# One-core two-block network in fp32 halves: two stage ends rebuilt and 1/sqrt by a polynomial

## The chip, the cores and the metric

One core of a Trainium2 chip runs the whole network, one launch per execution. The metric is the device time of one execution in microseconds (us). Engines are named as in the profile: PE is the matrix engine and PEld its weight loads, DVE the vector engine, ACT the scalar engine, POOL the general one; SP only issues transfers.

## The reference, cut to what matters

The input is x of 512 positions by 1024 channels. First block, two layers of: RMS norm, one projection, three mixers (axial attention, pooling, window attention), gates, an output projection; then RMS norm, up projection, 3-tap convolution, gated product, down projection. Second block: a conformer convolution module with its feed-forward, then keys and values for a dilated attention, that attention and its feed-forward. What the change touches is the norms and the ends of two stages:

```python
def rms_norm(x, g):
    y = x * lax.rsqrt(jnp.mean(x * x, axis=-1, keepdims=True) + EPS)
    return y * g

def conformer_conv_module(h, w_in, b_in, dw, dw_b, ln_g, ln_b, w_out, b_out):
    u = h @ w_in + b_in
    u = u[..., :D_MODEL] * jax.nn.sigmoid(u[..., D_MODEL:])
    u = causal_dwconv(u, dw, dw_b)          # 31 taps, one filter per channel
    u = jax.nn.silu(layer_norm(u, ln_g, ln_b))
    return u @ w_out + b_out
...
# every stage: x = x + rms_norm(y, post_gain); h = rms_norm(x, pre_gain)
```

## The kernel before, in words

Every matrix product is made of three PE passes: both operands are split into a high half (an ACT copy, line 301 for weights) and a remainder (a DVE subtraction, line 302), and the passes are high by high, high by remainder, remainder by high (`mm3`, lines 345 to 347, weights standing; `mm3_rows`, lines 555 to 557, activations standing). A pass over 512 columns follows the one before it after about 0.23 us. Weights come in units of eight 128 by 128 tiles in the order of a list (`PLAN`): SP loads a unit into one of three `raw` buffers (line 269), `split_to` splits it two units ahead of its use into one of four `w` buffers, or, for the units that a closing uses twice, into a `keep` buffer that a stage lends (`keeper`). `queue_behind` puts the splits of kept units behind an instruction that a stage has named for that engine in `self.behind`; `self.hold` is the first kept unit that may not be split yet.

The instructions are emitted by a planner: `mm3` and its like advance a clock by their planned time (`spend`), and generators (`spawn`, `tick`) put their work in when the clock has passed what they yielded (`CONV_TAP`, `NORM_SUM`, `NORM_NEXT` and so on). The framework then orders each engine's list once more before the program is built, by what it holds to be ready, with emission as the priority; at run time each engine works down its list in order and waits where an operand is missing.

`closing` ends a stage in two halves of 256 rows. After the products of half 0 the generator `norms` runs the post norm (squares on ACT, line 403; `rms`, lines 396 and 397; `inv_sqrt`, lines 367 to 373; the residual, line 432) and `pre_norm` the next norm (four squares, `rms`, `xn` on ACT and DVE, lines 473 and 477, then the transposes `htp`, line 488, and the split into `hh` and `hl`), while PE has half 1 to do; then `head` multiplies half 0 of the next stage while half 1 is normed. `inv_sqrt` is one guess from the bits of the value and three Newton steps, ten DVE instructions in a chain; `rms` puts two before them. `rope` uses `inv_sqrt` too. The last closing has `last_norm` for each of its last two row tiles: add (line 449), square (403), gain over 1024 columns in place (451), `rms`, result (454) and the transfer out. At the start there is no matrix product before the first `pre_norm`: two squares per row tile, `rms`, `xn`, `htp`.

The conformer's first part (`conv_inputs`): 16 projections give eight tiles of channels. Tiles 0 to 2 are convolved on DVE by 30 multiply-adds each (`tap_sums`, line 1325; the last one writes `vc`), emitted `CONV_TAP` apart. Tiles 3 to 7 go to PE (`conv`): the gated product `cu` (line 1293) is spread by 16 small transfers (line 1301) into `cup`, 72 matmuls (line 1349) run in four quarters `i`, DVE adds the bias into `vc` (line 1359), and after a yield of 1.5 four transposes (line 1366) turn it; an ACT copy (1369) and four `bn_stats` (1373) follow. When all eight tiles have their statistics: `bn_aggr` (1378), variance plus epsilon (1382), `inv_sqrt`, the shift (1384), the normalization of four row tiles of 1024 columns, two on ACT (1389) and two on DVE (1393). `silu_tiles` then transposes each tile of channels back (`ltp`, line 1236), applies Silu on ACT (`ct`, line 1241) and splits it into `ch` and `cl` for the closing `cm_w_out`.

The dilated attention (`dilated`, `dilated_heads`): eight heads; the first four units of the closing `w_o` are multiplied by `close_begin` while the last head is still worked on; the four kept units get their buffers from a pool that is opened after the heads' own pool is closed.

Of the kernel before, what the change touches and what calls it, by code (L numbers as in the profile page):

```python
# [35 lines left out]
DIN = 5888  # L36
EPS = 1e-6
NEG = -1e30
UNIT = 8
# [5 lines left out]

CONV_DVE, CONV_TAP = 3, 1.0
AX_LANES, AX_SOFTMAX, AX_NEXT, AX_PROB = 2, 5.5, 2.0, 1.7
# [177 lines left out]
class Kernel:  # L225
# [136 lines left out]
    def inv_sqrt(self, y, v):  # L362

        nc = self.nc
        shape = list(v.shape)
        a = self.sm.tile(shape, F32, tag="nwa", name="nwa", bufs=4)
        nc.vector.tensor_scalar(
            y.bitcast(I32), v.bitcast(I32), -0.5, 1597463007.0, op0=OP.mult, op1=OP.add
        )
        for _ in range(3):  # L370
            nc.vector.tensor_tensor(a, y, y, op=OP.mult)
            nc.vector.scalar_tensor_tensor(a, a, -0.5, v, op0=OP.mult, op1=OP.mult)
            nc.vector.scalar_tensor_tensor(y, a, 1.5, y, op0=OP.add, op1=OP.mult)

# [15 lines left out]
    def rms(self, sums):  # L390

        nc = self.nc
        n = sums.shape[1]
        v = self.sm.tile([P, 2], F32, tag="var", name="var", bufs=2)[:, :n]
        y = self.sm.tile([P, 2], F32, tag="rst", name="rst", bufs=4)[:, :n]
        nc.vector.tensor_tensor(v, sums[:, :, 0], sums[:, :, 1], op=OP.add)
        nc.vector.tensor_scalar(v, v, 1.0 / D, EPS, op0=OP.mult, op1=OP.add)
        self.inv_sqrt(y, v)
        return y

    def square(self, x, total):
        junk = self.sp.tile([P, S], F32, tag="junk", name="junk")
        self.nc.scalar.activation(junk, x, AF.Square, accum_out=total)  # L403

# [38 lines left out]
    def last_norm(self, t, banks, y, gain):  # L443

        nc = self.nc
        sums = self.sm.tile([P, 2, 2], F32, tag="sums", name="sums", bufs=4)[:, :1]
        halves = [(y[:, t, n * S : (n + 1) * S], slice(n * S, (n + 1) * S)) for n in range(2)]
        for n, (to, _) in enumerate(halves):
            nc.vector.tensor_tensor(to, to, banks[n], op=OP.add)
            self.square(to, sums[:, 0, n : n + 1])  # L450
        nc.vector.tensor_tensor(y[:, t], y[:, t], gain, op=OP.mult)
        rs = self.rms(sums)
        for n, (to, cols) in enumerate(halves):
            nc.vector.scalar_tensor_tensor(
                self.x[:, t, cols], to, rs[:, 0:1], self.x[:, t, cols], op0=OP.mult, op1=OP.add
            )
            queue = nc.scalar if n else nc.sync
            queue.dma_start(self.out[t * P : (t + 1) * P, cols], self.x[:, t, cols])

    def pre_norm(self, h, gain, wait=(0.0, 0.0)):  # L460
# [9 lines left out]
        for i in range(2):  # L470
# [5 lines left out]
            else:  # L476
                last = nc.scalar.activation(
                    xn[i], self.x[:, 2 * h + i], AF.Copy, scale=rs[:, i : i + 1]
                )
            if h == 0 and self.n_unit:  # L480
                self.behind[last.ins.engine] = last.ins
# [771 lines left out]
    def conv_inputs(self):  # L1253
# [54 lines left out]
        def tap_sums():  # L1308
            for j in range(CONV_DVE):
# [27 lines left out]
                summed.append(j)  # L1337

        def conv():
            for j in range(CONV_DVE, KD):  # L1340
# [5 lines left out]
                for i in range(4):  # L1346
                    w = mats[j][:, i]
                    for m in range(CONV_M):
# [4 lines left out]
                        )  # L1353
                    self.spend(CONV_M * 0.218)
                    yield 0.0
                if j + 2 < KD:
# [5 lines left out]
                )  # L1362
                yield 1.5
                pt = self.psum("a", "ctp")
                for i in range(4):
                    nc.tensor.transpose(pt[:, i * P : (i + 1) * P], vc[:, i], self.ident)
                self.spend(0.45)
                by = pt.rearrange("s (i q c) -> s q i c", i=4, q=4)
                nc.scalar.activation(
                    vt[:, :, j * P : (j + 1) * P].rearrange("s q (i c) -> s q i c", i=4), by, AF.Copy  # L1370
                )
                for q in range(4):
                    nc.vector.bn_stats(stats[:, q, j], by[:, q])
            while len(summed) < CONV_DVE:
                yield 0.3
            mv = self.sm.tile([P, 4, 2], F32, tag="lmv", name="lmv")
            for q in range(4):
# [8 lines left out]
            )  # L1386
            for q in range(4):
                if q % 2:
                    nc.scalar.activation(
                        vt[:, q], vt[:, q], AF.Identity, scale=rs[:, q : q + 1], bias=sh[:, q : q + 1]  # L1390
                    )
                else:
                    nc.vector.tensor_scalar(
                        vt[:, q], vt[:, q], mv[:, q, 0:1], rs[:, q : q + 1],
                        op0=OP.subtract, op1=OP.mult,
                    )

# [151 lines left out]
    def dilated(self):  # L1549
        with self.tc.tile_pool(name="dily", bufs=1, reuse_waits="tile") as yp:  # L1550
# [3 lines left out]
            gain = self.row(yp, "mix_post_g1")  # L1554
            begun = self.dilated_heads(xs)
            with self.tc.tile_pool(name="kept", bufs=1, side="right", reuse_waits="tile") as tp:
                self.keeper(tp, "wt", 4)
                y = tp.tile([P, 4, D], F32, tag="y", name="y")
                self.closing("w_o", 0, xs, y, gain, "ffn_pre_g1", begun=begun)

# [224 lines left out]
```

## Time and profile before

| what | us |
|---|---|
| median of 3 runs (lowest, highest) | 3178.2 (3178.11, 3181.9) |
| profiled execution, its time | 3177.36 |
| its span, first to last instruction | 3175.6 |
| granted clock of PE, mean over the span | 0.997 |

The profile lists for each engine what it did, and for each idle stretch of an engine what ended it. In a row of the timeline the columns are start, duration, engine, line, operation, output<-inputs, shapes, count, and in square brackets the idle time of the engine ahead of it and who ended that. Rows of one kind that follow each other are merged.

### The profile page before, as it was taken

What the parts mean: (1) busy time and instruction counts of PE and PEld (TensorE: products, weight loads), DVE (VectorE), ACT (ScalarE), POOL (GpSimd) and SP (SyncE); (2) the same over time, 40 slices, a digit from 0 to 9 for tenths busy, and PEclk for the clock granted to TensorE, in tenths of its full rate; (3) what the DMA queues carried; (4) which work ended last, traced back from release to release, by engine and by line L of the source; (5) the groups of instructions that cost most, each with busy time, mean ns of one, the idle gap of its engine ahead of it and who ended that gap; (6) DMA issues with size and microseconds to landing.
All of it is one profiled execution on the core that took longest, in us unless ns stands there. A gap on an engine that the chain in (4) does not pass through costs nothing. (4 is left out here: it accounts for less than half of the span.)

```text
span 3175.6 us, 40474 instructions
## 1 busy us (share of the span) xinstructions
PE 3103.4 (98%) x15764; PEld 2609.7 (82%) x15764; DVE 1828.9 (58%) x3337; ACT 1360.2 (43%) x2231; POOL 337.1 (11%) x350
## 2 busy tenths in 40 slices
PE   8999999999999999999999989999999999999998
PEld 7788888888878888888888878888888888888887
DVE  6778346455676754555556865456545545464555
ACT  5566244334456643444334244334533333353332
POOL 0211100000011111000000000000143333100000
PEclk9999999999999999999999999999999999999999
DMA  4222232333311223233324422333222222223332
GB/s 139 67 77 84 94 106 85 95 100 94 99 64 60 90 90 107 79 100 98 95 93 161 152 87 73 97 95 120 74 87 73 75 86 80 74 87 99 95 99 73
DMA packets 86543, 293.84 MB, mean 93 GB/s; under 512 B 11088, under 2 KB 13904, under 8 KB 86352
## 3 DMA queue, kind: packets, MB, share of 16 engines
q1 hardware_dynamic: 82896, 278.41, 27.4%
q10 hardware_dynamic: 3456, 12.85, 1.1%
q8 instruction: 124, 2.03, 0.3%
q14 instruction: 67, 0.55, 0.0%
HBM read 287.81 MB, written 2.10 MB: 91 GB/s over the span
## 5 line engine op out<-in xcount | busy, mean ns | idle before, releaser
L345 PE MATMUL mm<-hh,w 128*128 128x512 f32 (+1 forms) x2720 | 1051.3, 386 | 0.0
L347 PE MATMUL mm<-hh,w 128*128 128x512 f32 (+1 forms) x2720 | 1035.7, 381 | 0.0
L346 PE MATMUL mm<-hl,w 128*128 128x512 f32 (+1 forms) x2720 | 1035.0, 381 | 0.0
L302 DVE TENSOR_TENSOR w<-raw,w 128x1024 fp32r<-128x1024 f32 x436 | 570.4, 1309 | 431.0 <-ACT w L301 426.4
L347 PEld LDWEIGHTS mm<-hh,w 128*128 128x128 f32 x2720 | 511.6, 188 | 97.0 <-issue 1.9
L346 PEld LDWEIGHTS mm<-hl,w 128*128 128x128 f32 x2720 | 512.4, 188 | 89.7 <-issue 1.9
L345 PEld LDWEIGHTS mm<-hh,w 128*128 128x128 f32 x2720 | 512.1, 188 | 89.8 <-issue 1.9
L301 ACT ACTIVATE w<-raw 128x1024 fp32r<-128x1024 f32 x436 | 458.5, 1053 | 236.8 <-PE mm L557 172.1
L679 DVE SCALAR_TENSOR_TENSOR cg<-mm,vecs,cg 128x511 f32<-128x511 f32 (+1 forms) x176 | 131.9, 749 | 207.0 <-ACT cg L672 204.3
L557 PE MATMUL mm<-w,al 128*128 128x512 f32 x576 | 224.7, 390 | 0.0
L555 PE MATMUL mm<-w,ah 128*128 128x512 f32 x576 | 224.6, 390 | 0.0
L556 PE MATMUL mm<-w,ah 128*128 128x512 f32 x576 | 224.6, 390 | 0.0
L679 DVE SCALAR_TENSOR_TENSOR cv<-mm,vecs,cv 128x511 f32<-128x511 f32 (+1 forms) x176 | 131.9, 749 | 103.9 <-ACT cv L672 101.2
L282 POOL TENSOR_TENSOR raw<-raw,vecs 128x1024 f32<-128x1024 f32 x66 | 132.7, 2012 | 545.4 <-DMA raw<-in_wall 503.7
L672 ACT ACTIVATE cg<-mm,vecs 128x512 f32<-128x512 f32 x88 | 68.6, 780 | 276.8 <-PE mm L347 276.8
L424 POOL TENSOR_TENSOR y<-y,row 128x512 f32<-128x512 f32 x18 | 23.3, 1311 | 1385.8 <-ACT junk L403 1385.8
L346 PE MATMUL mm<-hl,keep 128*128 128x256 f32 x512 | 144.9, 285 | 0.7 <-DVE hl L729 0.4
L347 PE MATMUL mm<-hh,keep 128*128 128x256 f32 x512 | 144.6, 284 | 0.0
L345 PE MATMUL mm<-hh,keep 128*128 128x256 f32 x512 | 143.2, 285 | 0.0
L555 PEld LDWEIGHTS mm<-w,ah 128*128 128x128 f32 x576 | 108.1, 188 | 23.2 <-issue 0.8
L556 PEld LDWEIGHTS mm<-w,ah 128*128 128x128 f32 x576 | 108.1, 188 | 22.4
L557 PEld LDWEIGHTS mm<-w,al 128*128 128x128 f32 x576 | 108.2, 188 | 22.2
(292 smaller groups left out, 4374.3 us busy)
## 6 DMA issues: line engine op xcount, KB each, us to landing
raw<-in_wall SPq DMA_DIRECT2D x500, 512.0 KB, 3.5
cw<-in_cm_mats ACTq DMA_DIRECT2D x20, 576.0 KB, 6.5
row<-in_rows SPq DMA_DIRECT2D x9, 512.0 KB, 4.3
bias<-in_rpb SPq DMA_DIRECT2D x16, 256.0 KB, 3.6
x<-in_x SPq DMA_DIRECT2D x4, 512.0 KB, 5.9
cup<-cu SPq DMA_DIRECT2D x80, 16.0 KB, 1.8
out<-x SPq DMA_DIRECT2D x4, 256.0 KB, 2.1
out<-x ACTq DMA_DIRECT2D x4, 256.0 KB, 2.1
```

Of the source, the lines that this page charges most:

```text
L282: self.nc.gpsimd.tensor_tensor(rows, rows, g[:, k0 : k0 + ks, None].to_broadcast(list(rows.shape)), op=OP.mult)
L301: nc.scalar.activation(hi, raw, AF.Copy),
L302: nc.vector.tensor_tensor(lo, raw, hi.bitcast(F32), op=OP.subtract),
L345: nc.tensor.matmul(ps, wh, xh, start=first and i == 0, stop=False, **check)
L346: nc.tensor.matmul(ps, wh, xl, start=False, stop=False, **check)
L347: nc.tensor.matmul(ps, wl, xh, start=False, stop=stop, **check)
L424: nc.gpsimd.tensor_tensor(to, to, gain[:, cols], op=OP.mult)
L555: nc.tensor.matmul(ps, xh, wh, start=first, stop=False)
L556: nc.tensor.matmul(ps, xh, wl, start=False, stop=False)
L557: nc.tensor.matmul(ps, xl, wh, start=False, stop=last)
L672: nc.scalar.activation(o, ps, AF.Identity, scale=self.vec(taps + str(k0), f), bias=self.vec(cb, f))
L679: nc.vector.scalar_tensor_tensor(o[:, to], ps[:, of], self.vec(taps + str(k), f), o[:, to], op0=OP.mult, op1=OP.add,)
```

## The change

- `inv_sqrt`: the same guess y, then w = 0.7235 v y², a polynomial of degree four in w by three multiply-adds, and y times that: seven DVE instructions. `square` scales by 1/sqrt(1024) inside the ACT instruction, so `rms` needs one instruction ahead of `inv_sqrt`.
- `last_norm`: the gain goes into a tile of its own, half by half, straight after the half's add.
- `pre_norm`: at the start too, the DVE splits of kept units are queued behind the DVE `xn`.
- `conv`: the transposes, copy and statistics of tile j go behind the second quarter of tile j+1's matmuls; 36 transposes into a spare bank and one early Silu on a single column stand ahead of `bn_aggr`; the normalization is made in halves of 512 columns, two on ACT and six on DVE, and kept units are split behind it. `CONV_TAP` goes from 1.0 to 0.9.
- `dilated`: the first kept unit gets a buffer of its own that exists before the heads begin, and may be split during them.

```diff
-CONV_DVE, CONV_TAP = 3, 1.0
+CONV_DVE, CONV_TAP, WARM = 3, 0.9, 36
 def inv_sqrt(self, y, v):
-        for _ in range(3):
-            nc.vector.tensor_tensor(a, y, y, op=OP.mult)
-            nc.vector.scalar_tensor_tensor(a, a, -0.5, v, op0=OP.mult, op1=OP.mult)
-            nc.vector.scalar_tensor_tensor(y, a, 1.5, y, op0=OP.add, op1=OP.mult)
+        nc.vector.tensor_tensor(w, y, y, op=OP.mult)
+        nc.vector.scalar_tensor_tensor(w, w, ISQRT_LEAD, v, op0=OP.mult, op1=OP.mult)
+        term = w
+        for c in ISQRT[:-1]:
+            nc.vector.scalar_tensor_tensor(q, term, c, w, op0=OP.add, op1=OP.mult)
+            term = q
+        nc.vector.scalar_tensor_tensor(y, q, ISQRT[-1], y, op0=OP.add, op1=OP.mult)
 def rms(self, sums):
-        nc.vector.tensor_tensor(v, sums[:, :, 0], sums[:, :, 1], op=OP.add)
-        nc.vector.tensor_scalar(v, v, 1.0 / D, EPS, op0=OP.mult, op1=OP.add)
+        nc.vector.scalar_tensor_tensor(
+            v, sums[:, :, 0], EPS, sums[:, :, 1], op0=OP.add, op1=OP.add
+        )
 def last_norm(self, t, banks, y, gain):
             self.square(to, sums[:, 0, n : n + 1])
-        nc.vector.tensor_tensor(y[:, t], y[:, t], gain, op=OP.mult)
+            scaled.append(self.sp.tile([P, S], F32, tag="xn", name="scaled", bufs=4))
+            nc.vector.tensor_tensor(scaled[n], to, gain[:, n * S : (n + 1) * S], op=OP.mult)
 def pre_norm(self, h, gain, wait=(0.0, 0.0)):
-            if h == 0 and self.n_unit:
+            if h == 0 and (self.n_unit or i):
                 self.behind[last.ins.engine] = last.ins
 def conv():
                     self.spend(CONV_M * 0.218)
+                    if i == 1 and waiting:
+                        by_token(*waiting.pop())
                     yield 0.0
...
-                yield 1.5
-                pt = self.psum("a", "ctp")
...
+                waiting.append((j, vc))
+            yield 1.5
+            by_token(*waiting.pop())
             while len(summed) < CONV_DVE:
                 yield 0.3
+            early = cv.tile([P, 1], F32, tag="early", name="early")
+            nc.scalar.activation(early, vc[:, 0, :1], AF.Silu)
+            spare = self.psum("b", "warm")
+            for _ in range(WARM):
+                nc.tensor.transpose(spare[:, :P], vc[:, 0], self.ident)
...
-            for q in range(4):
-                if q % 2:
...
+            for n in range(2):
+                for q in range(4):
+                    part = vt[:, q, n * S : (n + 1) * S]
+                    if q % 2 and n == 0:
+                        last = nc.scalar.activation(
+                            part, part, AF.Identity, scale=rs[:, q : q + 1], bias=sh[:, q : q + 1]
+                        )
+                    else:
+                        last = nc.vector.tensor_scalar(
+                            part, part, mv[:, q, 0:1], rs[:, q : q + 1],
+                            op0=OP.subtract, op1=OP.mult,
+                        )
+                    self.behind[last.ins.engine] = last.ins
 def dilated(self):
-            begun = self.dilated_heads(xs)
-            with self.tc.tile_pool(name="kept", bufs=1, side="right", reuse_waits="tile") as tp:
-                self.keeper(tp, "wt", 4)
+            with self.tc.tile_pool(name="kept1", bufs=1, side="right", reuse_waits="tile") as op:
+                count = [0]
+                def place():
+                    first = count[0] % 4 == 0
+                    count[0] += 1
+                    pool, tag, bufs = (op, "wt1", 1) if first else (self.tp, "wt", 3)
+                    w = pool.tile([P, 4, S], F32R, tag=tag, name="keep", bufs=bufs)
+                    return w.rearrange("p a b -> p (a b)")
+                self.keep, self.hold = place, HEADS[6] - 3
+                begun = self.dilated_heads(xs)
+                with self.tc.tile_pool(name="kept", bufs=1, side="right", reuse_waits="tile") as tp:
+                    self.tp = tp
...
```

## Rows read from the trace of the kernel before

**Rows 1.** The page's busy time: share of the span and count, the line of PE.

```profile
PE 3103.4 (98%) x15764; PEld 2609.7 (82%) x15764; DVE 1828.9 (58%) x3337; ACT 1360.2 (43%) x2231; POOL 337.1 (11%) x350
```

**Rows 2.** PE's waits: who waited, for whom, us in total, times, longest us.

```profile
PE htp L488 <- ACT xn L477: 26.6, 15, 13.9
PE ltp L1236 <- DVE vt L1393: 8.8, 1, 8.8
...
PE sc L914 <- DVE rrs L811: 2.8, 2, 1.4
...
PE mm L555 <- ACT keep L301: 2.5, 1, 2.5
```

**Rows 3.** Timeline of the start, all engines.

```profile
7.45 0.16 DVE L396 TENSOR_TENSOR var<-sums 128x2 f32<-128x2 f32 x1 [6.58 <-ACT junk L403]
...
9.37 1.23 DVE L302 TENSOR_TENSOR keep<-raw,keep 128x1024 fp32r<-128x1024 f32 x1 [0.77 <-ACT keep L301]
9.55 1.06 ACT L301 ACTIVATE keep<-raw 128x1024 fp32r<-128x1024 f32 x1 [0.21 <-DMA raw<-in_wall]
...
12.50 0.16 DVE L373 SCALAR_TENSOR_TENSOR rst<-nwa,rst 128x2 f32<-128x2 f32 x1
```

**Rows 4.** Timeline of the convolution's end, all engines.

```profile
1803.45 11.02 SPq L1301 DMA_DIRECT2D cup<-cu  x16
...
1810.27 0.66 PE L1366 MATMUL ctp<-ident,vc 128*128 128x128 f32 x4 [1.92 <-DVE vc L1359]
1810.76 8.20 PE L1349 MATMUL conv<-cup,cw 128*128 128x128 f32 x72
...
1819.00 0.69 DVE L1359 TENSOR_TENSOR vc<-conv,cbias 128x512 f32<-128x512 f32 x1 [6.52 <-PE conv L1349]
1819.61 2.05 DVE L1325 SCALAR_TENSOR_TENSOR vc<-cw,vecs,cacc 128x512 f32<-128x512 f32 x2
...
1823.91 1.05 DVE L1378 BATCH_NORM_AGGREGATE lmv<-stats 128x2 f32<-128x48 f32 x4
...
1830.47 2.38 ACT L1389 ACTIVATE vt<-vt,lsh,lrs 128x1024 f32<-128x1024 f32 x2 [4.57 <-DVE lsh L1384]
...
1833.81 1.28 ACT L1241 ACT_TABLE_LOAD   x1
...
1835.11 2.29 ACT L1241 ACTIVATE ct<-ltp,vecs 128x512 f32<-128x512 f32 x2
...
1838.22 0.78 PE L555 MATMUL mm<-w,ch 128*128 128x512 f32 x1
```

**Rows 5.** The page's DMA issues: count, KB each, median us to landing.

```profile
cup<-cu SPq DMA_DIRECT2D x80, 16.0 KB, 1.8
```

**Rows 6.** Stretches: busy us and count of each engine, PEclk, DMA share, GB/s.

```profile
1731.00:1810.00 79.00, 77.35 (x495) 69.15 (x493) 77.51 (x116) 17.15 (x23) 0.37 (x3) 1.00 0.47 159
```

**Rows 7.** The same view, the convolution's end.

```profile
1820.00:1823.00 3.00, 1.66 (x12) 1.00 (x10) 3.00 (x10) 1.73 (x4) 0.00 (x0) 1.00 0.00 0
...
1826.00:1830.00 4.00, 0.00 (x0) 0.00 (x0) 3.95 (x8) 0.00 (x0) 0.00 (x0) 0.54 0.37 94
...
1838.00:1840.00 2.00, 2.00 (x7) 1.69 (x6) 1.18 (x2) 2.00 (x3) 0.00 (x0) 0.51 0.01 2
```

**Rows 8.** Timeline of two closings: the wait ahead of half 0's transposes.

```profile
464.55 0.66 PE L488 MATMUL htp<-ident,xn 128*128 128x128 f32 x4 [0.96 <-ACT xn L477]
...
835.54 0.66 PE L488 MATMUL htp<-ident,xn 128*128 128x128 f32 x4 [0.94 <-ACT xn L477]
```

**Rows 9.** Timeline of the dilated closing, ACT.

```profile
2761.78 2.94 ACT L301 ACTIVATE keep<-raw 128x1024 fp32r<-128x1024 f32 x3
```

**Rows 10.** Timeline of the end, DVE.

```profile
3167.60 1.23 DVE L451 TENSOR_TENSOR y<-y,row 128x1024 f32<-128x1024 f32 x1 [0.85 <-ACT junk L403]
3168.74 0.15 DVE L396 TENSOR_TENSOR var<-sums 128x1 f32<-128x1 f32 x1
...
3170.86 0.16 DVE L373 SCALAR_TENSOR_TENSOR rst<-nwa,rst 128x1 f32<-128x1 f32 x1
```

More of the change, by code (lines that the diff above doesn't have):

```diff
@@ L37 @@
 EPS = 1e-6
+ISQRT_LEAD = 0.7235090067876623
+ISQRT = (-3.722972040482227, 5.656401103535527, -4.544375901094603, 2.4629594646252917)
 NEG = -1e30
@@ L365, in inv_sqrt @@
         shape = list(v.shape)
-        a = self.sm.tile(shape, F32, tag="nwa", name="nwa", bufs=4)
+        w = self.sm.tile(shape, F32, tag="nwa", name="nwa", bufs=4)
+        q = self.sm.tile(shape, F32, tag="nwq", name="nwq", bufs=4)
         nc.vector.tensor_scalar(
@@ L402, in square @@
         junk = self.sp.tile([P, S], F32, tag="junk", name="junk")
-        self.nc.scalar.activation(junk, x, AF.Square, accum_out=total)
+        self.nc.scalar.activation(junk, x, AF.Square, scale=D**-0.5, accum_out=total)
     def norms(self, h, banks, y, add, gain, bias, pre):
@@ L446, in last_norm @@
         sums = self.sm.tile([P, 2, 2], F32, tag="sums", name="sums", bufs=4)[:, :1]
+        scaled = []
         halves = [(y[:, t, n * S : (n + 1) * S], slice(n * S, (n + 1) * S)) for n in range(2)]
@@ L450, in last_norm @@
             self.square(to, sums[:, 0, n : n + 1])
-        nc.vector.tensor_tensor(y[:, t], y[:, t], gain, op=OP.mult)
+            scaled.append(self.sp.tile([P, S], F32, tag="xn", name="scaled", bufs=4))
+            nc.vector.tensor_tensor(scaled[n], to, gain[:, n * S : (n + 1) * S], op=OP.mult)
         rs = self.rms(sums)
-        for n, (to, cols) in enumerate(halves):
+        for to, (n, (_, cols)) in zip(scaled, enumerate(halves), strict=True):
             nc.vector.scalar_tensor_tensor(
@@ L1337, in tap_sums, with by_token @@
                 summed.append(j)
+        waiting = []
+        def by_token(j, vc):
+            pt = self.psum("a", "ctp")
+            for i in range(4):
+                nc.tensor.transpose(pt[:, i * P : (i + 1) * P], vc[:, i], self.ident)
+            self.spend(0.45)
+            by = pt.rearrange("s (i q c) -> s q i c", i=4, q=4)
+            nc.scalar.activation(
+                vt[:, :, j * P : (j + 1) * P].rearrange("s q (i c) -> s q i c", i=4), by, AF.Copy
+            )
+            for q in range(4):
+                nc.vector.bn_stats(stats[:, q, j], by[:, q])
         def conv():
@@ L1362, in conv @@
                 )
-                yield 1.5
-                pt = self.psum("a", "ctp")
[L1365 to L1371, printed above, removed]
-                for q in range(4):
-                    nc.vector.bn_stats(stats[:, q, j], by[:, q])
+                waiting.append((j, vc))
+            yield 1.5
+            by_token(*waiting.pop())
             while len(summed) < CONV_DVE:
                 yield 0.3
+            early = cv.tile([P, 1], F32, tag="early", name="early")
[3 more added lines that the diff above has]
+                nc.tensor.transpose(spare[:, :P], vc[:, 0], self.ident)
             mv = self.sm.tile([P, 4, 2], F32, tag="lmv", name="lmv")
@@ L1386, in conv @@
             )
-            for q in range(4):
-                if q % 2:
[L1389 to L1396, printed above, removed]
+            for n in range(2):
+                for q in range(4):
+                    part = vt[:, q, n * S : (n + 1) * S]
[7 more added lines that the diff above has]
+                            op0=OP.subtract, op1=OP.mult,
+                        )
+                    self.behind[last.ins.engine] = last.ins
         matrices(CONV_DVE)
@@ L1554, in dilated @@
             gain = self.row(yp, "mix_post_g1")
-            begun = self.dilated_heads(xs)
-            with self.tc.tile_pool(name="kept", bufs=1, side="right", reuse_waits="tile") as tp:
-                self.keeper(tp, "wt", 4)
-                y = tp.tile([P, 4, D], F32, tag="y", name="y")
-                self.closing("w_o", 0, xs, y, gain, "ffn_pre_g1", begun=begun)
+            with self.tc.tile_pool(name="kept1", bufs=1, side="right", reuse_waits="tile") as op:
[10 more added lines that the diff above has]
+                    self.tp = tp
+                    y = tp.tile([P, 4, D], F32, tag="y", name="y")
+                    self.closing("w_o", 0, xs, y, gain, "ffn_pre_g1", begun=begun)
     def dilated_heads(self, xs):
```

## The prediction

> **What bounds the kernel now.** I read the page's busy times first: PE is busy for 98% of the span [rows 1], so time can only be won where PE stands still, and every microsecond of other engines' work that PE doesn't wait for is worth nothing. The second view is the list of PE's waits [rows 2], which says where those 2% are. One wait of 13.9 us is the start. Fourteen more on the same pair hold 26.6 - 13.9 = 12.7 us, 0.9 each, two for each of the seven closings that lead into a next stage. One of 8.8 us is the end of the conformer's convolution; 2.5 us are the dilated closing's, 2.8 us the axial stage's, two waits in all. The reader is to see that PE's losses are a few serial chains, and that what shortens such a chain counts in full. The third view is the timeline at each of these places [rows 3, 4, 8 to 10], to see what the chain is made of. What follows the last matmul is such a chain too, though PE's waits don't list it.
>
> **The change, part by part.** *The price of a small DVE instruction.* At the end, 12 of them in a chain start 3168.74 to 3170.86 [rows 10]: 2.12 / 11 = 0.193 us from one to the next. A root with its two preparations goes from 12 to 8, so 0.77 us; the layer norm's and the rope's root from 10 to 7, so 0.58.
>
> *The end.* The gain of 1024 columns begins only when the square has read y (3167.60) and holds the chain for 1.14 us until the sum [rows 10]. In a tile of its own, half of it runs while ACT squares. Gain 1.14 + 0.77 = 1.9 us, bounds 1.6 to 2.1.
>
> *The start.* The root's chain begins at 7.45 and ends at 12.66, 5.21 us, for 12 x 0.193 = 2.3 us of work: two remainders of kept weights, of 1.23 us each, stand among its steps and wait for ACT's copy first [rows 3]. Behind `xn`, and with eight steps, it ends at 7.45 + 1.54 = 9.0. ACT has a copy until 9.34 and may do the second, until 10.61, before `xn`; so `xn` starts at 9.4 to 10.6 in place of 12.7, 2.1 to 3.3 us earlier. Behind it the squares of the other half and the remainders of kept units, now 0.5 us later, take part back: bounds 1.0 to 3.3, I take 2.0.
>
> *The convolution's end.* I follow the chain [rows 4]. (a) The last tile's matmuls wait 1.92 us for the transposes of the tile before, which move behind their second quarter. They cannot gain all of it: their input comes in 16 small transfers issued from 1803.45 to 1814.47 and landing 1.8 us later [rows 5], the last at 1816.3; the fourth quarter now starts at 1810.76 + 6.15 - 1.92 + 0.5 (the transposes moved in) = 1815.5 and waits 0.8. Gain 1.1. (b) The last two taps of DVE (2.05 us) stand behind the bias add of the last tile, ahead of its statistics, while DVE was idle for 6.52 us just before. Emitted 0.1 earlier per tap, 90 taps come 9 us of planned time sooner, more than that idle stretch. Gain 2.05, or 0 if the order leaves them there. (c) From `bn_aggr` to the ACT normalization go 1830.47 - 1823.91 = 6.56 us, in which three remainders of kept weights stand among the root's steps, each like those of the start [rows 3]. Without them: 1.05 + 9 x 0.193 = 2.8 (`bn_aggr`, the variance, seven of the root, the shift), and 0.1 to cross to ACT. Gain 3.65. (d) ACT normalizes two half tiles in place of two whole ones, 2.38 us halved: gain 1.1. DVE's two halves are done by then. (e) Between that and the first Silu lie 1835.11 - 1832.85 = 2.26 us, a kept copy and the table load of 1.28. With the table loaded by the early Silu, what is left is the first four transposes, 0.7 to 1.1: gain 1.4. (f) PE's clock: full until 1826, then 1.2 GHz to nearly 1840 [rows 7], so the closing's first 1.8 us ran at half speed. If the 36 transposes (72 matmuls of that width take 8.20 us, so 4.1) fill the gap, PE stands still for about 2 us: gain 0.9. Sum of (a) to (f): 10.2 us. Low bound 6.3, without (b), (f) and the rest of (a); high bound 11.1. PE has nothing else to do in this stretch, so the 4.1 us of transposes cost nothing as long as the normalization ends after them; by these steps it does, by 1 to 2 us. The four kept units split behind the normalization are needed four products after the closing's first, over 10 us later: nothing.
>
> On (f) the rows bear as follows: from 1820 to 1823 PE's only work was twelve transposes, 1.66 us, at full clock; it was at 1.2 GHz only after 1826, with no PE work in between [rows 7]. So transposes, even sparse ones, are followed by a clock that still stands. The Trainium skill (TensorE: Matmul & The Clock Gate, Part 4: PE-mode transpose) says that a transpose does not count as work for the clock in the way a matmul does. By it (f) would be 0 and the transposes in (e) some 0.5 us longer; the trace speaks against it as far as it goes, but has no 4 us of transposes alone. The Trainium skill (ScalarE: Activation LUTs, What ACT_TABLE_LOAD costs) prices a table switch at about 2.7 us; the row has 1.28 with the next instruction 0.02 behind it [rows 4], and the row decides: by that page of the Trainium skill (e) would be 1.4 larger.
>
> *The dilated closing.* PE waits 2.5 us for the first kept copy, since its buffer exists only after the heads. Three copies start at 2761.78, 0.98 apart [rows 9]. With the first unit split before, PE goes on at about 2761.78 + 1.0 - 2.5 = 2760.3 and asks for the second at 2763.0 (12 passes of 0.23 later), which now takes the first one's place and is copied by 2762.8, its remainder a little over 1 us later. Gain 2.2; bounds 1.5 to 2.5. The split moved ahead costs ACT 1.05 and DVE 1.2 us in a stretch in which both mostly idle.
>
> *The fourteen waits of the closings.* Two closings of different make have 0.96 and 0.94 us [rows 8]: wherever the chain ends, PE's list has the transposes about a microsecond too early. So their place follows the chain in the framework's order, and shortening the chain by two roots, 1.5 us, shortens the wait only by what the order doesn't see of it. Bounds: 0 each, if the place moves by as much; all 0.9, if it doesn't move. Nearest is what rows 8 show, so 0.2 each, 2.8 us in all, bounds 0 to 12.7.
>
> *The rope.* Two waits of 1.4 on `rrs` [rows 2] have root steps ahead of them on DVE. Two or three fewer: 0.4 each, 0.8 us; bounds 0 to 2.8.
>
> *At nothing.* The other roots lie beside PE's work; if PE came to wait there, they would cost less than before. The scale in the square and the moved transposes of earlier tiles are the same work.
>
> Sum: 1.9 + 2.0 + 10.2 + 2.2 + 2.8 + 0.8 = 19.9 us. The profiled execution took 3177.4, 1.8 over its span and 0.8 under the median of the runs. 3177.4 - 19.9 = 3157.5, and against the median 3158.3; I say 3158.5.
>
> **The rivals.** *DVE late in the convolution.* From 1731 to 1810 DVE is busy for 77.5 of 79 us [rows 6]. If the taps that come sooner get ahead of the last `cu`, up to nine of 0.75 us, then its 16 transfers and the last tile's matmuls come that much later: 6.75 us. For: no slack on DVE there. Against: PE was not held by DVE in that stretch, and DVE's whole work fits with 6.5 us to spare. Time 3158.5 + 6.75 = 3165.2.
>
> *Transposes don't keep the clock.* Then (f) is lost, and the first transposes and Silu run behind a slow PE: 0.9 + 0.9 = 1.8 us, 3160.3. For: no row has transposes alone for as long. Against: the stretch of twelve above.
>
> *The places don't move.* Then the fourteen waits vanish: 9.9 more, 3148.6. For: nothing but that the planner's numbers are unchanged. Against: rows 8.
>
> *The order undoes the edits*, with splits again between the root's steps and the taps where they were: the convolution's end gives only (a), (d) and (e), 3.6 in place of 10.2, and the start 0.8, the dilated closing nothing: 3158.5 + 6.6 + 1.2 + 2.2 = 3168.5, and within no change if the rope and the closings give nothing either.
>
> *Slower.* If the framework counts a small instruction at far more than 0.193, it moves the transposes ahead by more than the chain shrinks. Eight steps fewer per chain at a counted 0.45 would move them 3.6 us for 1.5, and each of the fourteen waits grows by 2.1: 3158.5 + 2.8 + 29 = 3190. It turns to slower than before at a growth of 1.2 per wait. For: the place does follow a count. Against: the waits of 0.95 say that the count is short of the chip, not over it.
>
> **How the numbers follow.** 0.62 for the forecast, 0.13 for DVE late, 0.12 for the clock, 0.07 for places that don't move, 0.03 for edits undone, 0.03 for slower. A measurement of this kernel can tell about 0.2%, 6.4 us, from no change: faster ends at 3171.8. Faster: all but the last two cases, less a little of the second, 0.92. Same 0.05, slower 0.03. The range takes in the forecast's own bounds (3153 to 3164), DVE late with its spread, and half of the case of 3148.6: 3149 to 3169.
>
> **What would show it.** In the changed profile: PE's first work at about 11 to 12 us; no `keep` remainder among root steps at the start and in the convolution's end; the last `ltp` wait gone and the closing's first matmul about 10 us nearer to the last convolution matmul than the 19.3 of before; PEclk full throughout that stretch; no wait of `mm` on `keep` in the dilated closing; the last gain multiplied before the last square ends. The sum is wrong if the fourteen waits total under 5 or over 15 us, or if PE waits for `cup` by more than 2 us.

## The result and the profile after

The changed kernel takes 3155.6 us, the median of four runs (3152.2 to 3156.6), beside 3179.7 for the kernel before (four runs): ratio 0.9922, 95% interval 0.9904 to 0.9939. The forecast was 3158.5. The profiled execution took 3156.3, its span is 3154.2, 21.4 us less than before; the terms of the forecast added up to 19.9. In this profile the total is near, but several terms are not, and they cancel. By the medians the gain is 24.2 us, so the sum was some 4 us short.

Busy time and PE's waits of the changed kernel, answering to [rows 1, 2] (who waited, for whom, us in total, times, longest):

```profile
PE 3105.9 (98%) x15800; PEld 2613.3 (83%) x15800; DVE 1804.2 (57%) x3178; ACT 1360.4 (43%) x2232; POOL 340.4 (11%) x350
```
```profile
PE htp L499 <- ACT xn L488: 18.3, 13, 10.7
PE htp L499 <- DVE hl L740: 8.9, 13, 1.7
PE qks L809 <- ACT rsq L804: 2.4, 2, 1.2
...
PE ltp L1247 <- DVE vt L1421: 1.3, 1, 1.3
...
PE sc L925 <- DVE rrs L822: 0.9, 1, 0.9
```

Without the start, 18.3 - 10.7 = 7.6 us are left of the closings' 12.7. The wait for `keep` is gone, the one for the normalized `vt` fell from 8.8 to 1.3. Two more rows of the kernel before, for what follows:

```profile
PE htp L488 <- DVE hl L729: 7.5, 7, 1.5
...
PE rot L803 <- ACT rqg L794: 2.0, 2, 1.0
```

To see where the rest went, I took the moments at which both kernels have done the same PE work (matmul by matmul, without the spare transposes) and subtracted them. I call the difference the lag; negative is earlier. A row of the table is what the lag gained or lost in that stretch. The third column is the same kernel in a second profiled execution (e9 below).

| stretch (time of before) | forecast | after | again |
|---|---|---|---|
| start, to 43 us | -2.0 | +1.2 | -1.7 |
| seven closings and two ropes (43 to 1728, 1842 to 2750, 2780 to 2860) | -3.6 | -10.1 | -10.0 |
| convolution's end (1728 to 1842) | -10.2 | -7.7 | -9.3 |
| dilated closing's kept copies (2750 to 2780) | -2.2 | -2.8 | -2.8 |
| last norm (2860 to the end) | -1.9 | -1.9 | -1.9 |
| sum | -19.9 | -21.4 | -25.7 |

The convolution's end after, timeline of all engines, answering to [rows 4]:

```profile
1807.05 4.18 PE L1374 MATMUL conv<-cup,cw 128*128 128x128 f32 x36
...
1811.27 0.69 DVE L1386 TENSOR_TENSOR vc<-conv,cbias 128x512 f32<-128x512 f32 x1 [2.50 <-PE conv L1374]
1811.88 2.07 DVE L1336 SCALAR_TENSOR_TENSOR vc<-cw,vecs,cacc 128x512 f32<-128x512 f32 x2
...
1816.20 1.04 DVE L1404 BATCH_NORM_AGGREGATE lmv<-stats 128x2 f32<-128x48 f32 x4
...
1819.12 1.52 ACT L1417 ACTIVATE vt<-vt,lsh,lrs 128x512 f32<-128x512 f32 x2 [3.76 <-DVE lsh L1410]
...
1821.49 2.30 ACT L1252 ACTIVATE ct<-ltp,vecs 128x512 f32<-128x512 f32 x2
...
1824.28 0.50 PE L566 MATMUL mm<-w,ch 128*128 128x512 f32 x1
```

From `bn_aggr` to the normalization there are now 2.92 us in place of 6.56, from there to the first Silu 2.37 in place of 4.64. The two last taps still stand behind the bias add, with 2.50 us of idle DVE ahead of it.

The clock in the same stage, stretches (busy us and count of PE, PEld, DVE, ACT, POOL, then PEclk, DMA share, GB/s), answering to [rows 7]:

```profile
1822.00:1824.00 2.00, 0.81 (x5) 0.58 (x6) 1.07 (x2) 2.00 (x3) 0.00 (x0) 1.00 0.08 14
1824.00:1826.00 2.00, 2.00 (x9) 1.66 (x9) 1.54 (x3) 2.00 (x3) 0.00 (x0) 0.66 0.76 248
1826.00:1828.00 2.00, 2.00 (x7) 1.52 (x6) 1.70 (x2) 2.00 (x4) 0.00 (x0) 0.50 0.00 0
```

Full through the spare transposes and up to 1824, then 1.2 GHz from 1824.6 to 1828.1, just as the closing begins: 3.4 us at half speed, about 1.5 lost by the table (-7.7 here, -9.3 in e9, which has no such spell there). The start, timeline, answering to [rows 3]; the last rows are PE alone, where the same transposes show the clock:

```profile
7.40 0.16 DVE L404 SCALAR_TENSOR_TENSOR var<-sums 128x2 f32<-128x2 f32 x1 [6.54 <-ACT junk L412]
...
8.78 0.16 DVE L381 SCALAR_TENSOR_TENSOR rst<-nwq,rst 128x2 f32<-128x2 f32 x1
...
10.72 1.97 PE L499 MATMUL htp<-ident,xn 128*128 128x128 f32 x8 [10.72 <-ACT xn L488]
...
16.34 0.84 PE L499 MATMUL htp<-ident,xn 128*128 128x128 f32 x3
...
19.18 0.49 PE L499 MATMUL htp<-ident,xn 128*128 128x128 f32 x3
```

The root's chain ends at 8.94, no remainder among its steps, and PE starts 3.2 us earlier than before. But three transposes still take 0.84 at 16.3 and 0.49 only at 19.2: PE ran at 1.2 GHz until 19.0, 6.3 us after its first real matmul (12.64), where the kernel before needed 1.6 (15.63 to 17.2).

### The profile page after: what moved, and what is told of

Read it like the earlier page. It is cut to its first block, busy times and chain, and to the rows that moved or that the text cites. A ratio compares the mean times of both kernels' runs of the same rounds, so it can differ in the third digit from the quotient of the medians.

```text
span 3154.2 us, 40406 instructions
## 1 busy us (share of the span) xinstructions
PE 3105.9 (98%) x15800; PEld 2613.3 (83%) x15800; DVE 1804.2 (57%) x3178; ACT 1360.4 (43%) x2232; POOL 340.4 (11%) x350
## 4 chain that ended last, share of the span: by engine, by line
PE 85%; DVE 7%; ACT 4%; DMA 2%; issue 1%; POOL 0%; SPq 0%; DVEq 0%; ACTq 0%; POOLq 0%
PE mm L348 19%; PE mm L350 19%; PE mm L349 19%; PE mm L566 5%; PE mm L568 5%; PE mm L567 5%; ACT junk L412 2%; DVE w L305 2%; DMA raw<-in_wall 2%; PE z L348 1%; PE z L349 1%; PE z L350 1%; PE conv L1374 1%; PE pt L937 1%; ACT w L304 1%
```

## The experiments

**The roots, taken out and alone.** e1 is the changed kernel with the old roots, e12 the old kernel with nothing but the new ones.

```diff
-        nc.vector.tensor_tensor(w, y, y, op=OP.mult)
...
-        nc.vector.scalar_tensor_tensor(y, q, ISQRT[-1], y, op0=OP.add, op1=OP.mult)
+        for _ in range(3):
+            nc.vector.tensor_tensor(a, y, y, op=OP.mult)
...
```

> The changed kernel with the three Newton steps, the two-instruction variance and the unscaled square put back; all else as changed. My theory: the roots are the cause of the shorter waits at the closings. In the changed kernel PE's waits of htp on ACT's xn hold 18.3 us, 10.7 of them the start, so 7.6 in the fourteen places; they return to about 12.7 (+5.1), the waits on rrs from 0.9 to 2.8 (+1.9), the end gets 0.8 longer, the start's first PE work 0.8 later, the convolution's root 0.6 longer: +9.2 us, 3164.8 against a median of 3155.6. Rival: the framework's place for the transposes follows the chain's length, and the waits shrank because the rest of the order changed: the fourteen stay at 7 to 9 us, and only the serial ends grow, by 0.8 + 0.8 + 0.6 and the rope's 0.6: +2.8, 3158.4.

> The kernel before with nothing but the shorter roots (polynomial, one-instruction variance, scaled square). My theory: the roots are worth in the waits of the closings what the run with the Newton steps lost, about 5, the rope 1 to 1.9, the end 0.8, the convolution's root 0.6 and one remainder fewer among its steps, 1.0, and the start 0 to 0.8: 8.4 to 10, 3169.5 to 3171. Rival, by the difference of medians of that run alone (6.35): 3173.

e1: 3161.9 (3161.2 to 3162.8), ratio 0.9944 (0.9928 to 0.9961). e12: 3165.8 (3163.2 to 3170.5), ratio 0.9959 (0.9945 to 0.9973). PE's waits, first of e1, then of e12:

```profile
PE htp L493 <- ACT xn L482: 24.3, 15, 11.4
...
PE sc L919 <- DVE rrs L816: 2.8, 2, 1.4
```
```profile
PE htp L496 <- ACT xn L485: 18.6, 13, 12.1
...
PE sc L922 <- DVE rrs L819: 0.9, 1, 0.9
```

With the old roots the closings' waits are 12.9 and the rope's 2.8, as in the kernel before; with the new ones alone 6.5 and 0.9. So the roots own these waits, the other edits nothing of them: theory one of e1 holds in its rows, and the rival falls. By equal PE work 1.9 of the 10.0 us at the closings and ropes stay with the old roots, and e1's time, 6.3 above the changed kernel's, lies between the two expectations (9.2 and 2.8). In time the roots are worth 13.7 us alone, outside both sizes expected of e12, and 6.3 where the rest is there, or 8.2 against e9, the same changed kernel measured again (3161.9 - 3155.6 and - 3153.7). Part of the difference is an overlap: alone, the shorter chain also lets only two remainders in among the convolution's root steps where the kernel before had three (6.56 became 4.96), and the hold does that work again; by equal PE work the roots bring 2.4 in that stage alone and 0.6 beside the rest. The larger part is at the closings and ropes, 12.5 in e12 against the 8.1 that e1 lost there; why they bring more alone stays open. The three remainders, timeline of the kernel before, DVE, then the two of e12:

```profile
1826.27 1.22 DVE L302 TENSOR_TENSOR keep<-raw,keep 128x1024 fp32r<-128x1024 f32 x1
...
1827.48 1.22 DVE L302 TENSOR_TENSOR keep<-raw,keep 128x1024 fp32r<-128x1024 f32 x1
...
1828.69 1.22 DVE L302 TENSOR_TENSOR keep<-raw,keep 128x1024 fp32r<-128x1024 f32 x1
```
```profile
1817.79 1.23 DVE L304 TENSOR_TENSOR keep<-raw,keep 128x1024 fp32r<-128x1024 f32 x1
1818.93 0.16 DVE L380 SCALAR_TENSOR_TENSOR lrs<-nwq,lrs 128x4 f32<-128x4 f32 x1
1819.00 1.22 DVE L304 TENSOR_TENSOR keep<-raw,keep 128x1024 fp32r<-128x1024 f32 x1
1820.14 0.16 DVE L1392 SCALAR_TENSOR_TENSOR lsh<-lmv,lrs 128x4 f32<-128x4 f32 x1
```

**The convolution's tail as before.**

```diff
-            spare = self.psum("b", "warm")
-            for n in range(2):
...
+            for q in range(4):
+                if q % 2:
```

> The changed kernel with the whole convolution stage of the kernel before (transposes behind each tile, whole-tile normalization on both engines, remainders not held behind it, no early Silu, no spare transposes, 1.0 per tap); roots, start, dilated closing and end as changed. By my reading the tail's edits without the root are worth 7.8 - 0.6 = 7.2 us of the lag at equal PE work: 3162.8, with the stretch from bn_aggr to the normalization back at about 6 us, the table load behind the normalization, and a wait of about 1.9 for the last tile. Rival: the three remainders among the root's steps cost most because there were three idle engine turns to fill, and with a shorter root fewer fit in: bn_aggr to normalization only 4 to 4.5 us, and the tail is worth 5 to 5.5 us: 3161.

One run, 3160.4, and `bn_aggr` to the normalization is 4.95: both nearer to the rival's (3161, 4 to 4.5) than to the theory's (3162.8, about 6). From the last convolution matmul to the closing's first go 17.97 us, 13.32 with the tail and 19.53 in the kernel before. The tail is worth 17.97 - 13.32 = 4.65 there, and 1.3 by the moved transposes (e7): 6.0 beside the shorter root. By equal PE work the stretch loses 7.9 against e9; the other 2 fit the clock, which in e3 stays at 1.2 GHz for the closing's first 4.2 us (half of it is 2.1).

**Single edits of the tail.** e6 leaves the remainders free, e7 puts the transposes back, e8 holds the last bias add behind the last taps.

```diff
-                    self.behind[last.ins.engine] = last.ins
```
```diff
-                    if i == 1 and waiting:
-                        by_token(*waiting.pop())
...
+                by_token(j, vc)
```
```diff
+                while j == KD - 1 and len(ends) < CONV_DVE:
+                    yield 0.1
...
+                    self.behind[add.ins.engine] = ends[-1]
+                    self.queue_behind([add])
```

> The changed kernel with one edit undone: the four remainders of the closing's kept units are not held behind the convolution's normalization. My step (c): three remainders of 1.2 us stood among the root's steps, so without the hold from bn_aggr's start to ACT's normalization go 2.9 + 3 x 1.0 to 1.2 = 5.9 to 6.5 us and the closing begins 3.0 to 3.6 later. Rival: with a root of eight steps only one remainder finds its place there (the order of the instructions has one, between the root and the shift), 2.9 + 1.2 = 4.1, and the closing begins 1.2 later; the hold is then worth 1.2 and the other 2.4 of (c) come from the shorter root and the halves.

> The changed kernel with the transposes of each convolution tile back behind their own tile, before the next one's matmuls; all else as changed. My step (a): PE waits for the bias add of the tile before, 1.9 us in the kernel before and 1.3 in the run with the whole tail of before, so the last convolution matmul comes 1.3 to 1.9 later against the work ahead of it, and so do the normalization and the closing: 3156.9 to 3157.5. Rival: DVE's last two taps and the statistics are the later end, behind a DVE that was busy all the time, so that the last matmul comes later but the normalization doesn't: closing's begin within 0.4, time 3155.6.

> The changed kernel with the last tile's bias add held behind the last two taps on DVE (the order that step (b) wanted from a smaller spacing, and that it did not bring). DVE stands idle 2.5 us before that bias add, and the two taps take 2.07. My theory: bn_aggr starts 1.6 to 2.1 earlier after the bias add (4.9 to about 3.0), and the closing's first matmul comes 1.3 to 2.1 earlier, less where the spare transposes (36, the last at 7.3 us after the last convolution matmul) now end last: 3153.5 to 3154.3. Rival: the tap tiles' own chain (transposes, copy, four statistics of each) ends before the last tile's anyway, so the statistics of the last tile stay last and what goes away is only DVE's 2.07 between them: the same gain, but if the taps start late, because the convolution tile before them holds DVE, the bias add is pushed back by up to 2 us and nothing is won: 3155.6 to 3157.6.

e6, 3153.2 (one run; its clock never fell), timeline, DVE:

```profile
1815.67 1.23 DVE L305 TENSOR_TENSOR keep<-raw,keep 128x1024 fp32r<-128x1024 f32 x1
1816.81 0.15 DVE L1410 SCALAR_TENSOR_TENSOR lsh<-lmv,lrs 128x4 f32<-128x4 f32 x1
```

One remainder, as the rival had it: 3.95 to the normalization in place of 2.92. The normalization to the first Silu is 1.94 in return, 0.4 less, so the stage is 13.94 long, 0.6 more. The hold's own worth is 0.6, where step (c) put 3.1 on it.

e7, 3156.1 (one run), timeline, PE:

```profile
1802.81 0.66 PE L1355 MATMUL ctp<-ident,vc 128*128 128x128 f32 x4 [1.10 <-DVE vc L1384]
1803.30 8.20 PE L1374 MATMUL conv<-cup,cw 128*128 128x128 f32 x72
```

The wait is back, the stage behind the last matmul is as long as in the changed kernel (13.31 and 13.32), and by equal PE work the stretch loses 1.3 against e9. So the moved transposes are worth about 1.3; the rival falls.

e8, 3154.7 (one run), timeline, DVE:

```profile
1805.45 2.05 DVE L1336 SCALAR_TENSOR_TENSOR vc<-cw,vecs,cacc 128x512 f32<-128x512 f32 x2
...
1812.74 0.69 DVE L1389 TENSOR_TENSOR vc<-conv,cbias 128x512 f32<-128x512 f32 x1 [2.50 <-PE conv L1375]
...
1816.20 1.04 DVE L1410 BATCH_NORM_AGGREGATE lmv<-stats 128x2 f32<-128x48 f32 x4
```

The taps stand 7 us ahead now, bias add to `bn_aggr` fell from 4.93 to 3.46, the stage from 13.32 to 11.84. That is the gain that step (b) wanted and the smaller spacing did not bring: with 1.0 per tap in place of 0.9 the changed kernel's instruction lists are the same on all five engines.

**The spare transposes.** e2 and e11 are the kernel without them, e9 the changed kernel once more, unaltered.

```diff
-CONV_DVE, CONV_TAP, WARM = 3, 0.9, 36
+CONV_DVE, CONV_TAP, WARM = 3, 0.9, 0
...
-            spare = self.psum("b", "warm")
```

> The changed kernel without the 36 spare transposes; they feed nothing of the output. In the changed kernel the last convolution matmul starts at 1810.96, the clock is full until 1824.6 and at 1.2 GHz from there to 1828.05, the closing begins at 1824.3. Theory one, the transposes held the clock: without them it falls some 7 us after the last convolution matmul, as in the kernel before (1818.7 to 1826), so at about 1818, all twenty transposes ahead of the first Silus run at half speed (0.5 us longer on the chain), and the closing begins at half speed and stays there for about 1.8 us or more: +0.5 and -0.8 to +0.9 against the changed kernel's own loss of 1.7, so 3155 to 3157. Theory two, transposes don't count for the clock: it falls where it fell with them, at 1824.6, and nothing moves: 3155.6.

> The changed kernel without the 36 spare transposes again, in five rounds, since one execution could not tell. In seven executions with them the clock fell once near this closing; in three without them (two kernels with the old tail among them) it fell each time, some 5 to 7.6 us after the last convolution matmul, and reached into the closing in two by 1.7 and 4.2 us, which cost 0.9 and 2.1 us. My theory: without them the median is 0.5 to 1.5 us higher than the changed kernel's, 3156 to 3157. Rival: the fall costs nothing, since PE has nothing to do until the closing and the clock is back by then: same median within 0.5, 3155.5.

> The changed kernel once more, unaltered, in five rounds beside the next two. In the profiled executions so far its own instruction lists gave 1.7 us more or less by one spell at 1.2 GHz (3.4 us long) after a wait of PE. My theory: the spells fall differently from execution to execution, so the median stays at 3154 to 3156, single runs spread over 4 us (3152 to 3157), and this profile need not have the spell at the closing's begin (1824.6 to 1828.1) or the late rise at the start (6.3 us after the first matmul). Rival: spell and late rise belong to the kernel, and both are here again, at the same places.

e2: 3154.7 (one run). e11: 3153.6 (3152.1 to 3154.9, five runs), ratio 0.9918 (0.9905 to 0.9932). e9: 3153.7 (3151.7 to 3155.1, four runs), ratio 0.9919 (0.9905 to 0.9932). The same stretches of e9 and then of e11:

```profile
1822.00:1824.00 2.00, 2.00 (x11) 1.58 (x10) 1.30 (x2) 2.00 (x4) 0.00 (x0) 1.00 0.08 33
```
```profile
1818.00:1820.00 2.00, 0.43 (x2) 0.26 (x3) 1.85 (x8) 0.94 (x2) 0.00 (x0) 0.50 0.00 0
1820.00:1822.00 2.00, 2.00 (x11) 1.79 (x11) 2.00 (x5) 2.00 (x3) 0.00 (x0) 0.50 0.00 0
...
1824.00:1826.00 2.00, 2.00 (x11) 1.47 (x11) 1.47 (x3) 2.00 (x3) 0.00 (x0) 1.00 0.62 233
```

Both theories of the clock were half right. The transposes hold it: in nine profiles with them it fell near the closing twice (the changed kernel's first, and e10), in the five without them every time. But the fall costs next to nothing here: in e2 and e11 it lasts 6.8 us, in which PE has only a few transposes, and is over at 1822.6 and 1823.9, before the closing's first matmul (1824.1, 1824.2). The stage is 13.28 and 13.32 long, as with them (13.32), and by equal PE work the stretch loses 0.2 against e9. With the long tail it reached into the closing, by 1.7 us in the kernel before, 4.2 in e3 and 2.1 in e12. What the edit bought is bought already by the shorter stage. In e9 neither the spell at the closing nor the late rise at the start (2.5 us after the first matmul) is there, but one at 919 us: the spells belong to an execution, not to the kernel.

**The dilated closing as before.**

```diff
-            with self.tc.tile_pool(name="kept1", bufs=1, side="right", reuse_waits="tile") as op:
...
+            begun = self.dilated_heads(xs)
```

> The changed kernel with the dilated closing's kept units as before (one pool made behind the heads); all else as changed. At this place the changed kernel gained 2.75 us of lag at equal PE work. Theory one: it is all the early place of the first unit: PE's wait for the first kept copy returns at 2.5 to 2.8 us, 3158.3. Theory two: the closing's two waits for the pre-norm shrank here by the root as at the other six closings (0.4 to 0.85 us at most of them), and the early unit is worth 2.0 to 2.3: 3157.7; the wait for the copy is then still 2.5 but the lag at this closing grows by only 2.0 to 2.3.

One run, 3156.6. The wait for `keep` is back, and by equal PE work the place loses 5.4 against the changed kernel: more than either theory, since the clock fell within the wait, to 1.2 GHz from 2741.7 to 2748.5 (the wait in PE's timeline, then the stretch 2742 to 2748, the columns as above):

```profile
2742.70 2.93 PE L566 MATMUL mm<-keep,dyh 128*128 128x512 f32 x6 [2.48 <-ACT keep L304]
```
```profile
2742.00:2748.00 6.00, 5.30 (x13) 4.15 (x14) 3.92 (x4) 3.13 (x4) 0.00 (x0) 0.50 0.48 150
```

Two other runs take the clock out of it. At this wait the lag drops by 2.75 in e1, with the old roots and the early unit, as in the changed kernel, and by 0.0 in e12, with the new roots and the units as before. So the early unit is worth 2.75 and the roots nothing at this place: theory one. What e4 loses beyond that, 2.6, is the spell, of whose 6.8 us the first 1.0 passes in the wait itself. The kernel before has the same wait without a spell, e12 has it with one of 3.4 us, which costs 1.5. A wait of that length may or may not cost the clock.

**The start.** e5 leaves the first remainders free; e10 puts 22 spare transposes ahead of the first work, and has e8's order.

```diff
-            if h == 0 and (self.n_unit or i):
+            if h == 0 and self.n_unit:
```
```diff
+            hot = self.psum("b", "hot")
+            for _ in range(22):
+                nc.tensor.transpose(hot[:, :P], self.ident, self.ident)
```

> The changed kernel with one edit undone: the remainders of the first kept units are not held behind the start's normalization. My theory: a remainder of 1.2 us comes back among the root's steps, PE's first work moves from 10.6 (10.3 to 10.8 in five runs) to 11.5 to 11.9, and by 41 us nothing of it is left, since the first steps are then held by the third unit of weights, which lands at 15.0 to 15.1 in every run whatever the root does, and by the conversions behind it: lag at equal PE work at 41 us against the kernel before within -1.3 to +1.2, as in the changed kernels so far. Rival: the hold is worth what the start gains, so that the lag at 41 us is 1.0 to 1.2 worse than in a changed kernel whose clock rose as soon after its first matmul, and the whole time 3156.7.

> The changed kernel with the last tile's bias add behind the last two taps, and with 22 spare transposes of the identity ahead of the first norm's transposes (they feed nothing of the output). The identity lands at 5.8 us, PE's first work is at 10.3 to 10.8, so the 22 (0.21 us each at 1.2 GHz) fill that gap. My theory: the clock is at 2.4 GHz by the first matmul or within 1 us of it, in place of 1.5 to 6.3 us behind it, which at half speed gives 0.7 to 3 us; of it the third unit's landing at 15.0 lets through at least half, and the taps give 1.5 as in their own run: 3152 to 3153.5 against the changed kernel's 3155.5, and a smaller spread. Rival: the start's time is set by the landing of the weights and by the conversions behind them (the wait of 1.1 to 1.9 for hl at 30 us just grows), so only the taps' 1.5 remain: 3154.

e5: 3154.3 (one run). PE's first work is at 12.23, later than expected, and at 43 us the lag is -0.5; the five profiles with the hold whose clock rose 1.7 to 2.5 us after the first matmul (e5: 1.5) have -1.3 to -1.7. The hold is worth about 1 us at 43 us, as the rival said, of the 1.6 to 2.3 by which PE starts earlier in those five; the rival's 3156.7 for the whole was not measured.

e10: 3151.4 (3149.3 to 3152.5, four runs), ratio 0.9911 (0.9898 to 0.9925). Timeline, PE:

```profile
5.75 4.96 PE L1672 MATMUL hot<-ident 128*128 128x128 f32 x22 [5.75 <-DMA ident<-in_ident]
10.73 1.09 PE L499 MATMUL htp<-ident,xn 128*128 128x128 f32 x8
```
```profile
12.66 0.50 PE L348 MATMUL mm<-hh,keep 128*128 128x256 f32 x2 [0.83 <-ACT hh L739]
```

The 22 run at 1.2 GHz (0.225 each), the eight behind them at 2.4 (0.12): the clock rises 2.0 us before the first matmul. But the transposes can't start before `xn` is there, and the first matmul still comes at 12.66, as in the changed kernel's first profile (12.64), since PE now waits 0.83 for ACT's `hh`. At 43 us the lag is -1.0, no better than the -1.3 to -1.7 of the profiles whose clock rose soon, so at the start the rival holds: the conversions set the time. e10's median is 2.3 below the changed kernel's beside it, of which the taps can explain 1.5 (e8), but the ratios' intervals overlap, and its profile has a spell of 3.4 us at the closing (1819.7 to 1823.1) that takes those 1.5 back (-9.3 in this stage, as in e9; e8 has -10.8). The best of the versions tried in several runs, by the medians; not apart from the changed kernel by the intervals.

## Why the prediction was right, and where it was not

*The end*: as worked out, 1.9 forecast and measured; e12 has 0.8 of it by the root alone, as the small instructions were priced. *(c)*: 6.56 to 2.92, 3.64 against 3.65; the size held, but its reason was mis-told. It put all three remainders on the hold, and e12 and e6 show that the shorter root alone brings 1.6 and the hold 1.0 of this piece; the last 1.0 comes with the rest of the tail's edits, which I did not split. *(d) and (e)*: the normalization to the first Silu fell by 2.27, forecast 2.5; behind it the closing's first matmul came 0.3 sooner, which I had not counted. *(a)*: about 1.3 by e7, forecast 1.1; PE did not wait for `cup` at all, where I had left 0.8. *The dilated closing*: 2.75 by equal PE work, all of it the early unit's, forecast 2.2 with a bound of 2.5; the small wait for the second copy that was taken off did not come.

*(b) failed*: "Emitted 0.1 earlier per tap, 90 taps come 9 us of planned time sooner". The spacing sets no place here, the taps stand behind the bias add in both kernels; only a dependence moved them (e8, 1.5 us). *(f)*: the transposes mostly hold the clock as forecast (it stayed in seven of nine profiles), and in e10 it rose at 10.67 behind nothing but transposes; but the 0.9 us were not theirs to win, since without them the fall ends before the closing (e11). The Trainium skill (TensorE: Matmul & The Clock Gate, Part 4: PE-mode transpose) has it that a transpose doesn't count as work for the clock in the same way as a matmul. For transposes as this kernel issues them, against the identity, these traces show the contrary: the 22 of e10 alone were followed by the rise, and the clock fell in all five profiles without the 36.

Of the signs named, two failed with these steps: the closing's first matmul came 6.2 us nearer to the last convolution matmul (13.3 in place of 19.5 from start to start), not 10, and the clock was not full throughout.

*The start* was the worst term in this profile: 2.0 forecast, 1.2 lost. Two things were missing. The clock rose late; in the executions with the hold where it rose within 2.5 us the start keeps 1.3 to 1.7. And PE waits 1.7 us for `hl`, where the kernel before waits 0.4. ACT's copy ahead of it waits for weights that land 2.2 us later than before; in e9 they land 0.7 earlier and the waits there are 1.1. Timeline before and after, ACT and PE:

```profile
28.51 1.06 ACT L301 ACTIVATE w<-raw 128x1024 fp32r<-128x1024 f32 x1 [0.19 <-DMA raw<-in_wall]
...
31.37 0.63 PE L488 MATMUL htp<-ident,xn 128*128 128x128 f32 x4 [0.38 <-DVE hl L729]
```
```profile
30.71 1.06 ACT L304 ACTIVATE w<-raw 128x1024 fp32r<-128x1024 f32 x1 [2.11 <-DMA raw<-in_wall]
...
33.57 0.63 PE L499 MATMUL htp<-ident,xn 128*128 128x128 f32 x4 [1.73 <-DVE hl L740]
```

The forecast for the start followed the root's chain alone and did not ask what the weights allow behind it. Why they land when they do I didn't trace.

*The fourteen waits* are the term that was sized furthest too small: the 0.2 each came from "their place follows the chain in the framework's order", and they lost 5.1 together in this profile and 5.5 in e9, nearly twice the 2.8. The mechanism holds: in PE's list half 0's transposes stand 3 to 5 matmuls earlier in every closing, and e1 puts them back. But the place follows by about three quarters only: each half's transposes have two roots ahead of them, 1.5 us, and the wait shrank by some 0.4 on average. It is uneven: half 0's waits went from 0.9 (0.55 in one) to 0.06 in two closings and to 0.4 to 0.6 in five, while at three closings half 1's transposes moved up by 18 and their wait grew from 0.8 to 1.0, the way that the rival *Slower* had it, though by 0.16 only. The waits of e9:

```profile
PE htp L499 <- ACT xn L488: 17.2, 13, 10.0
PE htp L499 <- DVE hl L740: 6.3, 12, 0.9
PE qks L809 <- ACT rsq L804: 2.4, 2, 1.2
```

In e9 PE's list explains 8.2 of the closings' and ropes' 10: these 5.5, 1.5 at the rope (2.8 for `rrs` and 2.0 for `rqg` became 0.9 for `rrs` and 2.4 for `rsq`), and 1.2 for `hl` (7.5 to 6.3); the rest is in stalls that I didn't trace. So in the first profile the total was right partly by luck, by misses that cancel: -3.2 at the start, -2.5 at the convolution, +6.5 at the closings, +0.6 at the dilated closing. In e9, without the late rise and the spell at the closing, the first two are -0.3 and -0.9, the closings' +6.4 is not made up for, and the gain is 25.7 in place of 19.9. None of the rivals happened as a whole; the one of places that don't move came nearest, with a part of its 9.9, and of the edits undone only the taps were.

## What to carry to other kernels

A small serial chain is worth its length wherever PE's list waits behind it, so count how often it is run before looking at where it is longest: the roots, 0.8 us a piece, brought at least as much as the whole rebuilt tail (without them the changed kernel loses 6.3 us, without the tail 4.8 in one run). Where a planner orders instructions, move one by a dependence and read the lists, since a changed due time may move nothing. And before a filler is put into an idle stretch to hold the clock, look whether the clock is back anyway before PE has real work: here the fall was over by then.

## What was not expected of the hardware

The clock rose 1.5 to 6.3 us after PE's first matmul in the thirteen profiles without spare transposes at the start, and 2.0 us before it in e10. Besides, single spells at 1.2 GHz, of 3.4 or 6.8 us, stand near 92, 919, 1679, 1820 or 2745 us, each behind waits of PE of 1.2 to 2.5 us, in some profiles and not in others with the same instructions there. By equal PE work one of 3.4 cost 1.5 us at 1825 and 2752 and about 0.5 at 92 and 919, and two profiles of one kernel (3154.2 and 3149.9 us of span) differ by 4.3, with two spells and the late rise in the one and a single spell in the other: a stage's loss in a single profile need not be the edit's.
